# Trailing the transposes of GpSimd's products by one unit, and moving the initial chunks' product to another PSUM bank and another engine, in a hybrid decoder block

## The chip, the core and the metric

One core of one Trainium2 chip runs the whole program in one launch, in float32. The metric is the device time of one execution in microseconds (us). The core has a matrix engine (TensorE, PE in the profile, with its weight loads as PEld), a vector engine (VectorE, DVE), an activation engine (ScalarE, ACT), a general-purpose engine (GpSimd, POOL) and an engine that only issues transfers here (SyncE, SP). Each engine works through its own instructions strictly in order and waits on semaphores for the others.

## The reference

The input `x` is 1 x 2048 x 1024. Sixteen learned meta tokens are put in front, and one layer is computed:

```
h    = concat(meta, x)
proj = rmsnorm(h) @ w_in                       # 1024 -> 1024, columns split in two
u    = proj[:, :512]   -> 32 groups x 16 ch    # S5: 64 complex states a group
v    = proj[:, 512:]   -> 4 groups x 128 ch    # trailing means over 2/4/8/16 positions
s_t  = A s_{t-1} + B u_t ;  y = Re(C s) + d*u  # per group, A diagonal and complex
ys   = gelu(y) * sigmoid(gelu(y) @ glu_w + glu_b)
yp   = ((mean_w(v) - v) @ pool_w) * pool_scale
h    = h + concat(rmsnorm(ys), rmsnorm(yp)) @ w_out
h    = h + (silu(n2 @ w_gate) * (n2 @ w_up)) @ w_down      # n2 = rmsnorm(h), FF 2816
out  = rmsnorm(h), meta tokens dropped
```

## The kernel before

**Tiling.** The 2048 positions are two halves (`b` = 0, 1) of 128 chunks of T = 8 consecutive positions. A slice is one position of every chunk of a half: 128 rows, so there are 8 slices a half, and a 17th slice with the 16 meta tokens. In the program's text slices 1 and 2 are projected first, then slice 0 (the meta tokens), then 3 to 16. Products with large weights are made in float32r: each operand is split into a high and a low part (`split`, L107) and three matmuls stand for one (`mm3`, L116 to L119). So a line of the profile with `pj`, L117 to L119, is a matmul of the input projection.

**The recurrence.** The 32 S5 groups are handled in 8 units of 4 groups (`UG` = 4, `NU` = 8). With chunks of 8 positions, a unit needs four tables, which are built on the chip from the parameters and parked in DRAM as `pk_d[u]`, 2568 columns wide:

- columns 0 to 511: the matrices that lead from a chunk's inputs to its state. GpSimd multiplies them out (`ptp`, L551: two products and a sum in `outer`), TensorE transposes them (`pp`, L564), ScalarE copies the bank (`pst`, L566), SP sends it off (L567);
- columns 512 to 1023: `n9`, from the state to the outputs, multiplied out by VectorE (L550), sent off by L552;
- columns 1024 to 1535: the product within a chunk. TensorE makes `kp` from `n9` (L556), ScalarE copies it to `ks` (L559), VectorE adds the diagonal (L560), SP writes it to a padded array in DRAM (L561), and eight transfers read it back shifted (L569);
- the rest: cosines and sines `tb`, begun by four small GpSimd copies (L573 to L576) and doubled by VectorE in `grow` (L578).

That is `units()`. It is a generator, and so is `params()` ahead of it, which prepares the small parameter tables: `advance(2)` takes two steps of them before each slice of the first half (L633 to L639), so that TensorE has projections beside the building of the tables. All temporaries of `units()` have one buffer, but for `n9` and `tb` with two.

**The second stage.** When all tables are built, their SBUF is handed back (`par.close()`, L642), `pool_block(0)` forms the trailing means with GpSimd sums and one VectorE operation (L727) a group, and `ssm_unit(0, u)` runs the recurrence of one unit on the first half, unit by unit, while the 8 slices of the second half are projected (L734 to L740). In `ssm_unit`: load `pk` (L661); for the first half, the product of the two meta chunks, `pv0` (two columns a group, L677), copied by VectorE to `sm` (L678), combined into the initial state `z[:, :, 0]` (L679 to L681); then the product of the 128 chunks, `pvs` (L686); a rotation (L689), the scan (L691), a rotation back in which GpSimd takes two multiplications (L695), and the output product `py` (L700, L701), read by ScalarE with GELU (L704).

**Banks.** PSUM has eight banks in three rings: `tr` (2, transposes), `mm` (4, the projection and later matmuls) and `s` (2). In the first half `kp` and `pp` share the `s` ring; in the second stage `pv0`, `pvs` and `py` share it.

**The order of the work.** The program's text is not the order on the engines: before the launch a planner sorts each engine's instructions by their place in the text and by when its own cost model thinks that they are ready. That order is then fixed. A matmul that waits for another engine holds up every matmul that the planner put behind it.

Of the kernel before, what the change touches and what calls it, by code (L numbers as in the profile page):

```python
# [16 lines left out]
P = 128  # L17
# [5 lines left out]
H = 16  # L23
# [4 lines left out]
UG = 4  # L28
NU = G // UG
# [8 lines left out]
def kernel(  # L38
# [9 lines left out]
    V, A, GP, PE, SY = nc.vector, nc.scalar, nc.gpsimd, nc.tensor, nc.sync  # L48
# [9 lines left out]
    pk_d = [dram.tile([P, PKN], F32, name=f"pk_d{u}") for u in range(NU)]  # L58
# [13 lines left out]
    def tr_tile(nm):  # L72
        return ps_tr.tile([P, 4, P], F32, name=nm, tag="tr")

    def mm_tile(nm):
        return ps_mm.tile([P, 512], F32, name=nm, tag="mm")

    def s_tile(nm):
        return ps_s.tile([P, 512], F32, name=nm, tag="s")

    def g4(ap):
        return ap.rearrange("p (g k) -> p g k", g=UG)

    def tt(o, a, b, op, e=V):
        e.tensor_tensor(o, a, b, op=op)  # L85
# [36 lines left out]
    ident = const.tile([P, P], F32, name="ident")  # L122
# [29 lines left out]
    def yview(b):  # L152

        return xu[b].rearrange("c g t h -> c (g t h)").rearrange("c (k t e) -> c k t e", k=4, t=T)
# [352 lines left out]
    def grow(ct, st, w1, w2, n, ck, sk, e1, e2):  # L507

        lo, hi = slice(0, n), slice(n, 2 * n)
        sh = [P, ct.shape[1], n]  # L510
        ck = ck.unsqueeze(2).to_broadcast(sh)
        sk = sk.unsqueeze(2).to_broadcast(sh)
        w1, w2 = w1[:, :, :n], w2[:, :, :n]
        tt(ct[:, :, hi], ct[:, :, lo], ck, M_, e1)
        tt(w1, st[:, :, lo], sk, M_, e1)
        tt(ct[:, :, hi], ct[:, :, hi], w1, S_, e1)
        tt(st[:, :, hi], st[:, :, lo], ck, M_, e2)
        tt(w2, ct[:, :, lo], sk, M_, e2)
        tt(st[:, :, hi], st[:, :, hi], w2, A_, e2)
# [11 lines left out]
    def units():  # L531
        unit_p = par.enter_context(tc.tile_pool(name="unit", bufs=1))

        def pu_(shape, nm, bufs=None):
            return unit_p.tile(shape, F32, name=nm, tag=nm, bufs=bufs)

        for u in range(NU):
            gs = slice(u * UG, (u + 1) * UG)
            n9 = pu_([P, UG, 9, H], "n9", 2)
            n9t = pu_([P, UG, 9, H], "n9t")  # L540
            ptp = pu_([P, UG, 8, H], "ptp")
            ptt = pu_([P, UG, 8, H], "ptt")

            def outer(o, tmp, xp, xq, yp, yq, K, e):
                sh = [P, UG, K, H]
                tt(o, xp[:, gs, :K].unsqueeze(3).to_broadcast(sh), yp[:, gs].unsqueeze(2).to_broadcast(sh), M_, e)
                tt(tmp, xq[:, gs, :K].unsqueeze(3).to_broadcast(sh), yq[:, gs].unsqueeze(2).to_broadcast(sh), M_, e)
                tt(o, o, tmp, A_, e)

            outer(n9, n9t, xa1, xa2, zv[0], zv[1], 9, V)  # L550
            outer(ptp, ptt, xr1, xr2, y1, y2, 8, GP)  # L551
            SY.dma_start(pk_d[u][:, 512:1024].rearrange("p (g k) -> p g k", g=UG),  # L552
                         n9[:, :, 1:].rearrange("p g k h -> p g (k h)"))
            kp = g4(s_tile("kp"))
            for i in range(UG):
                PE.matmul(kp[:H, i], y1[:, u * UG + i], n9[:, i, :8].rearrange("p k h -> p (k h)"),  # L556
                          start=True, stop=True)
            ks = pu_([H, UG, P], "ks")
            A.copy(ks, kp[:H])  # L559
            tt(ks[:, :, :H], ks[:, :, :H], dg[:, gs], A_)  # L560
            SY.dma_start(kpad_d[gs, :, P:].rearrange("g h e -> h g e"), ks)  # L561
            pp = g4(s_tile("pp"))
            for i in range(UG):
                PE.transpose(pp[:, i], ptp[:, i].rearrange("p k h -> p (k h)"), ident)  # L564
            pst = pu_([P, UG, P], "pst")
            A.copy(pst, pp)  # L566
            SY.dma_start(pk_d[u][:, :512].rearrange("p (g k) -> p g k", g=UG), pst)  # L567
            for j in range(8):
                SY.dma_start(pk_d[u][j * H:(j + 1) * H, 1024:1536].rearrange("h (g k) -> h g k", g=UG),  # L569
                             kpad_d[gs, :, P - j * H:2 * P - j * H].rearrange("g h e -> h g e"))  # L570
            tb = pu_([P, 2, UG, NCH + 1], "tb", 2)
            tw = pu_([P, 2, UG, 64], "tw")
            GP.tensor_copy(tb[:, 0, :, :NE], eb[:, 0, gs])  # L573
            GP.tensor_copy(tb[:, 1, :, :NE], eb[:, 1, gs])
            GP.tensor_copy(tb[:, 0, :, NCH], cA[:, 8, gs])
            GP.tensor_copy(tb[:, 1, :, NCH], sA[:, 8, gs])  # L576
            for k in range(4, 7):
                grow(tb[:, 0], tb[:, 1], tw[:, 0], tw[:, 1], 1 << k, cA[:, k + 1, gs], sA[:, k + 1, gs], V, V)  # L578
            SY.dma_start(pk_d[u][:, 1536:], tb.rearrange("p q g c -> p (q g c)"))
            yield  # L580


    banks = [mm_tile(f"pj{q}") for q in range(4)]
# [64 lines left out]
    def rotate(o, tmp, vv, cc, sg, sign, eng=V):  # L648

        tt(o, vv, cc, M_)  # L650
        tt(tmp[:S], vv[S:], sg[S:], M_, eng)
        tt(tmp[S:], vv[:S], sg[:S], M_, eng)
        tt(o, o, tmp, A_ if sign > 0 else S_)
# [3 lines left out]
    def ssm_unit(b, u):  # L657
        g0 = u * UG
        gs = slice(g0, g0 + UG)
        pk = ss_p.tile([P, PKN], F32, name="pk", tag="pk", bufs=2)  # L660
        SY.dma_start(pk, pk_d[u])  # L661
        pm, nm, mm = g4(pk[:, :512]), g4(pk[:, 512:1024]), g4(pk[:, 1024:1536])
        ct, sg = g4(pk[:, 1536:2052]), g4(pk[:, 2052:2568])
        if u % 2 == 0:
            us8[0] = ss_p.tile([P, 2 * UG, NCH], F32, name="us", tag="us", bufs=2)
            for h in range(2):
                pu = tr_tile("put")
                for i in range(UG):
                    PE.transpose(pu[:, i], xu[b][:, g0 + h * UG + i].rearrange("c t h -> c (t h)"), ident)
                A.copy(us8[0][:, h * UG:(h + 1) * UG], pu)  # L670
        us = us8[0][:, (u % 2) * UG:(u % 2 + 1) * UG]
        z = ss_p.tile([P, UG, NCH + 1], F32, name="z", tag="z", bufs=2)
        sm = ss_p.tile([P, 4, UG], F32, name="sm", tag="sm", bufs=2)
        if b == 0:
            pv0 = g4(s_tile("pv0"))
            for i in range(UG):
                PE.matmul(pv0[:, i, :2], pm[:, i], um_sb[:, g0 + i], start=True, stop=True)  # L677
            V.tensor_copy(sm[:, 2:4], pv0[:, :, :2].rearrange("p g c -> p c g"))  # L678
            rotate(sm[:, 0], sm[:, 1], sm[:, 2], ct[:, :, 1], sg[:, :, 1], 1)  # L679
            tt(sm[:, 0], sm[:, 0], r8[:, gs], M_)  # L680
            tt(z[:, :, 0], sm[:, 0], sm[:, 3], A_)  # L681
        else:
            V.tensor_copy(z[:, :, 0], carry[:, gs])
        pv = g4(s_tile("pvs"))
        for i in range(UG):
            PE.matmul(pv[:, i], pm[:, i], us[:, i], start=True, stop=True)  # L686
        wr = ss_p.tile([P, UG, NCH], F32, name="wr", tag="wr")
        tmp = ss_p.tile([P, UG, NCH], F32, name="tmp", tag="tmp", bufs=2)
        rotate(wr, tmp, pv, ct[:, :, 1:], sg[:, :, 1:], -1)  # L689
        for i in range(UG):  # L690
            V.tensor_tensor_scan(z[:, i, 1:], r8[:, g0 + i:g0 + i + 1].to_broadcast([P, NCH]), wr[:, i],  # L691
                                 z[:, i, 0:1], op0=M_, op1=A_)
        st = ss_p.tile([P, UG, NCH], F32, name="st", tag="st")
        tmp2 = ss_p.tile([P, UG, NCH], F32, name="tmp2", tag="tmp", bufs=2)
        rotate(st, tmp2, z[:, :, :NCH], ct[:, :, :NCH], sg[:, :, :NCH], 1, GP)  # L695
        if b == 0:
            rotate(carry[:, gs], sm[:, 1], z[:, :, NCH], ct[:, :, NCH], sg[:, :, NCH], 1)
        py = s_tile("py")
        for i in range(UG):
            PE.matmul(py[:, i * P:(i + 1) * P], us[:, i], mm[:, i], start=True, stop=False)  # L700
            PE.matmul(py[:, i * P:(i + 1) * P], st[:, i], nm[:, i], start=False, stop=True)  # L701
        c0 = u % 2 * UG * H
        yv = yview(b)[:, u // 2][:, :, c0:c0 + UG * H].rearrange("c t (i h) -> c t i h", h=H)
        A.activation(yv, py.rearrange("c (i t h) -> c t i h", i=UG, t=T), AF.Gelu_apprx_tanh)  # L704
# [26 lines left out]
    for _ in pool_block(0):  # L731
        pass
    ssm_unit(0, 0)
    for u in range(NU):  # L734
        j = T + 1 + u
# [469 lines left out]
    g = 0  # L1205
# [60 lines left out]
```

## Time and profile before

| | |
|---|---|
| median of 3 executions (lowest to highest) | 1859.86 us (1859.7 to 1863.04) |
| the profiled execution | 1853.8 us |
| its span, first to last instruction | 1851.9 us |
| mean granted TensorE clock | 0.991 |
| busy: DVE, POOL, ACT | 1234.0, 813.3, 673.1 us |
| DMA | 298.36 MB, mean 161 GB/s |

The profile comes from one execution. A row of the timeline gives the start and length of an instruction, engine, line, what it writes and reads, and in square brackets how long the engine had been idle before it and whose end released it. A row of the waits gives engine, line and tile that waited, who ended the wait, the total in us, how often, and the longest. A row of the windows gives, for a stretch of the span, its length, the busy time (and count of instructions) of PE, PEld, DVE, ACT and POOL, the granted clock as a share of full speed, the DMA share and GB/s.

### The profile page before, as it was taken

What the parts mean: (1) busy time and instruction counts of PE and PEld (TensorE: products, weight loads), DVE (VectorE), ACT (ScalarE), POOL (GpSimd) and SP (SyncE); (2) the same over time, 40 slices, a digit from 0 to 9 for tenths busy, and PEclk for the clock granted to TensorE, in tenths of its full rate; (3) what the DMA queues carried; (4) which work ended last, traced back from release to release, by engine and by line L of the source; (5) the groups of instructions that cost most, each with busy time, mean ns of one, the idle gap of its engine ahead of it and who ended that gap; (6) DMA issues with size and microseconds to landing.
All of it is one profiled execution on the core that took longest, in us unless ns stands there. A gap on an engine that the chain in (4) does not pass through costs nothing.

```text
span 1851.9 us, 23672 instructions
## 1 busy us (share of the span) xinstructions
PE 1795.5 (97%) x8497; PEld 1491.6 (81%) x8497; DVE 1234.0 (67%) x1913; ACT 673.1 (36%) x1213; POOL 813.3 (44%) x619
## 2 busy tenths in 40 slices
PE   7999997999999999999999999999999999999998
PEld 6777886888887788888887788888888888888886
DVE  6995777766467876666667867776776444445763
ACT  5332334433455333333334333333333343333341
POOL 1774425633354465454657866665662000003400
PEclk9999998999999999999999999999999999999999
DMA  6355425444355344443436554554447765536771
GB/s 185 93 160 177 155 98 187 158 150 143 116 181 165 108 158 144 142 159 108 159 121 205 194 179 154 165 183 152 137 153 229 236 196 173 159 114 208 247 222 70
DMA packets 260517, 298.36 MB, mean 161 GB/s; under 512 B 17148, under 2 KB 204048, under 8 KB 255536
## 3 DMA queue, kind: packets, MB, share of 16 engines
q1 hardware_dynamic: 260304, 296.84, 50.5%
q8 instruction: 67, 1.10, 0.2%
q14 instruction: 50, 0.41, 0.1%
q0 software_dynamic: 96, 0.01, 0.0%
HBM read 202.37 MB, written 96.53 MB: 161 GB/s over the span
## 4 chain that ended last, share of the span: by engine, by line
PE 58%; issue 13%; DMA 7%; DVE 6%; POOL 3%; ACT 1%; POOLq 0%; SPq 0%; DVEq 0%; ACTq 0%
PE pr L117 13%; PE pr L118 13%; PE pr L119 13%; PE po L117 2%; PE po L119 2%; PE po L118 2%; PE pd L118 2%; PE pd L119 2%; PE pd L117 2%; DMA hd<-h_d 2%; DMA c<-c_d 1%; DVE wcl L85 1%; DMA out_dram<-c 1%; PE pj L119 1%; PE pj L117 1%
## 5 line engine op out<-in xcount | busy, mean ns | idle before, releaser
L85 DVE TENSOR_TENSOR wcl<-raw,wch 128x512 fp32r<-128x512 f32 x176 | 179.1, 1020 | 34.4 <-ACT wch L110 33.4
L110 ACT CAST wch<-raw 128x512 fp32r<-128x512 f32 x176 | 108.7, 622 | 255.2 <-PE pr L118 227.5
L85 DVE TENSOR_TENSOR fl<-fr,fh 128x512 fp32r<-128x512 f32 x168 | 115.1, 697 | 122.3 <-ACT fh L110 122.1
L110 ACT CAST fh<-fr 128x512 fp32r<-128x512 f32 x168 | 96.0, 584 | 193.1 <-PE pd L118 167.3
L110 ACT CAST wch<-s 128x512 fp32r<-128x512 f32 x132 | 82.0, 622 | 221.6 <-PE pr L118 168.7
L85 POOL TENSOR_TENSOR s<-raw 128x512 f32<-128x512 f32 x44 | 66.8, 1518 | 168.3 <-DVE wcl L85 74.1
L85 DVE TENSOR_TENSOR wcl<-s,wch 128x512 fp32r<-128x512 f32 x132 | 122.5, 928 | 23.2 <-ACT wch L110 23.1
L85 POOL TENSOR_TENSOR db22h<-db22h,hd 128x512 f32<-128x512 f32 x4 | 5.2, 1294 | 251.5 <-DVE db22h L85 251.5
L117 PE MATMUL po<-wh,mh 128*128 128x512 f32 x256 | 103.9, 406 | 2.9 <-ACT mh L767 2.9
L117 PE MATMUL pj<-wh,xh 128*128 128x512 f32 x256 | 103.3, 411 | 2.3 <-ACT xh L110 2.3
L118 PE MATMUL pj<-wl,xh 128*128 128x512 f32 x256 | 102.6, 403 | 0.0
L119 PE MATMUL pj<-wh,xl 128*128 128x512 f32 x256 | 102.4, 405 | 0.0
L119 PE MATMUL po<-wh,ml 128*128 128x512 f32 x256 | 100.7, 394 | 0.0
L118 PE MATMUL po<-wl,mh 128*128 128x512 f32 x256 | 100.7, 393 | 0.0
L85 POOL TENSOR_TENSOR rs<-rv,mhalf 128x1 f32<-128x1 f32 (+2 forms) x35 | 32.0, 914 | 152.6 <-DVE rv L91 143.4
L85 POOL TENSOR_TENSOR wr<-wr 128x512 f32<-128x512 f32 x44 | 67.0, 1523 | 66.8 <-DMA wr<-in_w_down_dram 61.3
L85 DVE TENSOR_TENSOR gt<-gt,ut 128x512 f32<-128x512 f32 x88 | 92.8, 1056 | 0.0
L85 POOL TENSOR_TENSOR ut<-gt 128x512 f32<-128x512 f32 x22 | 34.2, 1555 | 106.6 <-DVE gt L85 106.6
L85 POOL TENSOR_TENSOR tmp<-z,pk 64x512 f32<-64x512 f32 x32 | 49.0, 1531 | 71.4 <-issue 57.5
L85 DVE TENSOR_TENSOR gt<-pr,gt 128x512 f32<-128x512 f32 x66 | 45.4, 689 | 50.7 <-PE pr L119 50.3
L1017 ACT ACTIVATE gt<-gt 128x512 f32<-128x512 f32 x88 | 55.5, 632 | 53.4 <-DVE gt L85 53.4
L117 PE MATMUL pr<-xt2h,wch 128*128 128x512 f32 x176 | 68.8, 391 | 6.1 <-DVE gt L85 3.5
(394 smaller groups left out, 5550.8 us busy)
## 6 DMA issues: line engine op xcount, KB each, us to landing
fr<-ff_d SPq DMA_DIRECT2D x56, 704.0 KB, 5.0
raw<-in_w_gate_dram SPq DMA_DIRECT2D x44, 512.0 KB, 4.9
raw<-in_w_up_dram SPq DMA_DIRECT2D x44, 512.0 KB, 4.5
ff_d<-gt SPq DMA_DIRECT2D x22, 1024.0 KB, 3.9
pk<-pk_d SPq DMA_DIRECT2D x16, 1284.0 KB, 6.2
ff_d<-ut SPq DMA_DIRECT2D x22, 768.0 KB, 5.4
wr<-in_w_down_dram SPq DMA_DIRECT2D x22, 512.0 KB, 3.3
wd_d<-wr SPq DMA_DIRECT2D x22, 512.0 KB, 3.6
```

Source lines behind the costliest of these rows:

```text
L85: e.tensor_tensor(o, a, b, op=op)
L110: A.copy(hi, src)
L117: PE.matmul(o, lh, rh, start=first, stop=False)
L118: PE.matmul(o, lh, rl, start=False, stop=False)
L119: PE.matmul(o, ll, rh, start=False, stop=last)
L1017: lambda i, j: A.activation(gt[:, i, j], gt[:, i, j], AF.Silu), b == 0 and f0 == 0)
```

## The change

In `units()` the four transposes, the copy and the transfer of a unit's GpSimd product become a function `turn_p`. Unit u calls it for the product of unit u-1; the last product is turned after the loop, with one more step of the generator. For this the product `ptp` has two buffers in place of one. In `ssm_unit` the product of the meta chunks `pv0` takes a bank of the ring `mm` in place of `s`, and ScalarE copies it to `sm` in place of VectorE.

```
+        def turn_p(u, ptp):
+
+            pp = g4(s_tile("pp"))
+            for i in range(UG):
+                PE.transpose(pp[:, i], ptp[:, i].rearrange("p k h -> p (k h)"), ident)
+            pst = pu_([P, UG, P], "pst")
+            A.copy(pst, pp)
+            SY.dma_start(pk_d[u][:, :512].rearrange("p (g k) -> p g k", g=UG), pst)
+
+        was = None
         for u in range(NU):
...
-            ptp = pu_([P, UG, 8, H], "ptp")
+            ptp = pu_([P, UG, 8, H], "ptp", 2)
...
             SY.dma_start(kpad_d[gs, :, P:].rearrange("g h e -> h g e"), ks)
-            pp = g4(s_tile("pp"))
-            for i in range(UG):
-                PE.transpose(pp[:, i], ptp[:, i].rearrange("p k h -> p (k h)"), ident)
-            pst = pu_([P, UG, P], "pst")
-            A.copy(pst, pp)
-            SY.dma_start(pk_d[u][:, :512].rearrange("p (g k) -> p g k", g=UG), pst)
+            if u:
+                turn_p(u - 1, was)
+            was = ptp
...
             yield
+        turn_p(NU - 1, was)
+        yield
...
-            pv0 = g4(s_tile("pv0"))
+            pv0 = g4(mm_tile("pv0"))
...
-            V.tensor_copy(sm[:, 2:4], pv0[:, :, :2].rearrange("p g c -> p c g"))
+            A.copy(sm[:, 2:4], pv0[:, :, :2].rearrange("p g c -> p c g"))
```

## The prediction

> **What bounds the kernel now.** I read the page's first part, then the windows around the two places that the change touches, then TensorE's waits there, and only then single rows.
>
> ```profile
> span 1851.9 us, 23672 instructions
> PE 1795.5 (97%) x8497; PEld 1491.6 (81%) x8497; DVE 1234.0 (67%) x1913; ACT 673.1 (36%) x1213; POOL 813.3 (44%) x619
> ```
>
> TensorE is busy 97% of the span, so a gain must be idle or slow TensorE time. The stretches that matter are the building of the tables (60 to 142 us), what is left of the first half (142 to 158), the first units of the recurrence (158 to 211) and the rest of it (211 to 290):
>
> ```profile
> 60.00:142.00 82.00, 75.69 (x384) 59.82 (x384) 75.82 (x196) 28.89 (x50) 62.03 (x71) 0.95 0.49 146
> 142.00:158.00 16.00, 16.00 (x83) 13.38 (x81) 2.02 (x6) 4.28 (x8) 0.55 (x1) 1.00 0.55 164
> 158.00:211.00 53.00, 46.59 (x262) 39.53 (x261) 44.98 (x75) 16.69 (x28) 35.27 (x28) 0.97 0.46 163
> 211.00:290.00 79.00, 79.00 (x466) 68.93 (x467) 56.19 (x126) 25.80 (x42) 17.98 (x15) 1.00 0.31 111
> ```
>
> TensorE idles 6.31 us in the first stretch and 6.41 in the third, and not at all in the second and fourth, so what it has won by 211 us is kept to 290. But in the first stretch VectorE is busy 75.82 of 82 us and in the third 44.98 of 53: a second engine stands close behind TensorE in both places where TensorE waits. The waits, first from 60 to 160 us, then from 150 to 290:
>
> ```profile
> PE pp L564 <- POOL ptp L85: 6.3, 2, 5.0
> ```
>
> ```profile
> PE pvs L686 <- DVE sm L678: 5.8, 2, 3.4
> PE pv L677 <- POOL sum L85: 0.4, 1, 0.4
> ```
>
> The change aims at the first two. Together they are 12.1 us, 0.65% of the span.
>
> **Part one, the trailing transposes.** Per unit the same four transposes, one copy and one transfer remain; they move behind `kp` of the next unit on TensorE, behind the next `ks` copy on ScalarE, and on SP behind the unit's own eight `kpad_d` reads and its `tb`. What the removed wait was worth:
>
> ```profile
> 94.47 1.11 PE L564 MATMUL pp<-ident,ptp 128*128 128x128 f32 x4 [4.96 <-POOL ptp L85]
> 130.47 0.66 PE L564 MATMUL pp<-ident,ptp 128*128 128x128 f32 x4 [1.36 <-POOL ptp L85]
> ```
>
> ```profile
> 95.00:100.00 5.00, 5.00 (x16) 3.93 (x15) 3.09 (x3) 1.06 (x2) 4.92 (x4) 0.53 0.29 60
> ```
>
> After the 4.96 us gap the granted clock is 0.53 for the whole of the next five us, which loses 5 x 0.47 = 2.4 us (the four transposes there take 1.11 us, after the short gap 0.66). So the ceiling of this part is 4.96 + 2.4 + 1.36 = 8.7 us.
>
> Does GpSimd's product really come in time when the transposes trail? The late product and why it was late:
>
> ```profile
> 87.53 5.16 POOL L85 TENSOR_TENSOR ptp<-xr,y 128x512 f32<-128x512 f32 x1
> 92.77 1.66 POOL L85 TENSOR_TENSOR ptp<-ptp,ptt 128x512 f32<-128x512 f32 x1
> ```
>
> ```profile
> POOL ptp L85 <- PE pp L564: 7.5, 3, 4.1
> ```
>
> The product ended at 94.43 and `pp` started at 94.47. From unit 2's `pp` (94.47) to unit 6's (130.47) are 36 us, 9 a unit, so a product that is turned one unit later is ready even where it takes 5.16 us. GpSimd also loses its own 7.5 us of waiting for the single buffer. I take the whole wait as gone from `pp`, at no cost for the second buffer.
>
> What is late next? VectorE and, behind it, SP. VectorE's idle time in this stretch that GpSimd caused, the last table, and the way from it to the first `pk`:
>
> ```profile
> 100.61 0.23 DVE L85 TENSOR_TENSOR tb<-tb,cA 128x64 f32<-128x64 f32 x1 [2.49 <-POOL tb L573]
> 128.79 0.23 DVE L85 TENSOR_TENSOR tb<-tb,cA 128x64 f32<-128x64 f32 x1 [1.65 <-POOL tb L573]
> 129.21 1.29 DVE L85 TENSOR_TENSOR tb<-tb,cA 128x64 f32<-128x64 f32 x1
> 142.28 0.20 DVE L85 TENSOR_TENSOR ks<-ks,dg 16x64 f32<-16x64 f32 x1
> ```
>
> ```profile
> 145.07 0.38 SPq L561 DMA_DIRECT2D kpad_d<-ks  x1
> 149.17 5.00 SPq L569 DMA_DIRECT2D pk_d<-kpad_d  x8
> 154.29 0.51 SPq L661 DMA_DIRECT2D pk<-pk_d  x1
> ```
>
> ```profile
> 160.72 1.02 PE L677 MATMUL pv<-um_sb,pk 128*128 128x2 f32 x8 [0.41 <-POOL sum L85]
> ```
>
> The first `pk` is issued at 154.29 behind the last eight reads and is needed at 160.72, where TensorE already waits 0.41 us; the sums named there are no operand of this matmul, so I read it as the landing of `pk`. If TensorE arrives 8.7 us sooner and `pk` does not, it stands there. How much sooner can `pk` come? At most by VectorE's two waits, 2.49 + 1.65 = 4.1 us; at least 0, since SP issues without a pause from 149.17 to 154.29. I take 3, nearer the ceiling, because the 7.5 us that GpSimd no longer waits lie ahead of both `tb` copies. The trailing means need only the last slice of the first half, so their first sum and VectorE's first operation on it move into the empty 142 to 158 stretch, which keeps them out of the way of unit 0. Part one: 3 us, bounds 0 and 8.7.
>
> **Part two, `pv0`.** The rows at its two waits, TensorE's first and then VectorE's:
>
> ```profile
> 177.71 0.49 PE L686 MATMUL pvs<-us,pk 128*128 128x128 f32 x2 [2.46 <-DVE sm L678]
> 178.35 0.79 PE L701 MATMUL py<-pk,st 128*128 128x128 f32 x2 [0.15 <-DVE st L85]
> 181.49 0.91 PE L686 MATMUL pvs<-us,pk 128*128 128x128 f32 x6
> 210.83 1.16 PE L686 MATMUL pvs<-us,pk 128*128 128x128 f32 x8 [3.38 <-DVE sm L678]
> 211.82 0.60 PE L229 MATMUL ptv<-ident,vs 128*128 128x128 f32 x4
> ```
>
> ```profile
> 177.57 0.73 DVE L85 TENSOR_TENSOR st<-st,tmp 128x512 f32<-128x512 f32 x1
> 182.44 0.69 DVE L85 TENSOR_TENSOR wr<-pvs,pk 128x512 f32<-128x512 f32 x1 [1.52 <-PE pvs L686]
> 201.67 1.23 DVE L94 SCALAR_TENSOR_TENSOR pt<-sum,vt 128x1024 f32<-128x1024 f32 x1 [1.98 <-POOL sum L85]
> 210.69 0.68 DVE L85 TENSOR_TENSOR xl<-pt,xh 128x512 fp32r<-128x512 f32 x1
> ```
>
> With a bank of its own, `pv0` no longer stands before `pvs`. But in the same order the next matmul is `py` L701, which needs `st`, and VectorE ends that at 177.57 + 0.73 = 178.30. So the first wait mostly changes its name: TensorE does `pvs` in it (about 1 us) and then waits until 178.3. What is won is that `pvs` is done before `py` and not after it, so VectorE's 1.52 us before `wr` goes. At 210.83 the next in line is `ptv`, which needs a `tr` bank that VectorE's `xl` frees at 210.69 + 0.68 = 211.37; it started at 211.82, so 0.4 us are won of 3.38. The copies:
>
> ```profile
> L678 DVE COPY sm<-pv x8: 155/158/168, 161.8 to 269.3; 128x8 f32<-128x8 f32 x8
> ```
>
> ```profile
> L259 ACT COPY um_sb<-ptm x1: 213/213/213, 58.6 to 58.6; 128x64 f32<-128x64 f32 x1
> ```
>
> Eight copies of 0.158 us leave VectorE, three of them (units 1 to 3) in the stretch that it bounds: 0.5 us. ScalarE gets eight of at most 0.213, beside 16.69 busy us in 53; behind them wait evacuations of the projection. The bank taken from `mm` costs at worst that the projection waits out one such copy a unit, 8 x 0.213 = 1.7 us; no row shows TensorE waiting for that ring in these stretches, and the copy is released by TensorE's own last `pv0` matmul, so I take nothing. Part two: 1.5 + 0.4 + 0.5 = 2.4 us. Bounds: -1.7, and above all idle of both waits, 2.46 + 0.15 + 3.38 = 6.0, plus the slow clock after the first:
>
> ```profile
> 175.00:180.00 5.00, 2.39 (x12) 1.96 (x11) 4.81 (x14) 0.00 (x0) 4.11 (x4) 0.82 0.34 107
> 180.00:185.00 5.00, 5.00 (x27) 4.53 (x27) 3.42 (x5) 1.87 (x3) 4.13 (x4) 0.83 0.42 145
> ```
>
> The clock lost is 5 x 0.18 + 5 x 0.17 = 1.7 us: 7.7 in all. The Trainium skill, "TensorE: Matmul & The Clock Gate", section "HAM oscillation", wants idle gaps of more than about 3.4 us before the clock is halved: by it this wait of 2.46 us would have cost no clock and the ceiling would be 6.0; the trace agrees for the gap of 4.96 us and speaks against it here.
>
> **The sum.** 3 + 2.4 = 5.4 us. Against the profiled execution, 1853.8 (its span of 1851.9 and 1.9 around it), that gives 1848.4. The median of the runs is 6.1 above that execution, so I take the difference from the median: 1859.86 - 5.4 = 1854.5 us. What a measurement of this kernel tells from no change is about 0.2%, 3.7 us.
>
> **Rivals.**
>
> *The lead is swallowed (no change).* VectorE has 6.2 us to spare in the first 82, and part of its busy time is not work: the same `tb` form takes 0.23 us at 128.79 and 1.29 at 129.21, with GpSimd at work on a product. If GpSimd's earlier products only hold VectorE at other places, `pk` comes when it came, TensorE stands in front of `pv0` for what it won, and GpSimd's sums (the 1.98 us at 201.67) hold the third stretch. For it: VectorE's 75.82 of 82 us; against it: the 4.1 us are idle, not slow. It gives 0 to -2, about 1858.9. The Trainium skill, "SBUF — State Buffer", section "SBUF: two separate sides", has GpSimd and a VectorE operation with two SBUF inputs exclude each other for a whole instruction; by that rule earlier products win VectorE nothing, and this rival is the outcome. The 1.29 us agrees with it.
>
> *Everything counts.* The planner, with other arrival times, puts more projections in front of the first `pv0` and of `py`, and both waits vanish with their slow clock: 8.7 + 7.7 = 16.4, so 1843.5. Against it: `st` and `xl` are where the waits would move in the present order.
>
> *Slower.* The copy target `pst` still has one buffer. Products 6 and 7 are now turned close together, after unit 7's `kp`. The rows of unit 6's `pst` now, on ScalarE and SP:
>
> ```profile
> 131.21 0.59 ACT L566 COPY pst<-pp 128x512 f32<-128x512 f32 x1 [0.17 <-PE pp L564]
> 140.38 0.59 ACT L566 COPY pst<-pp 128x512 f32<-128x512 f32 x1 [0.39 <-DMA pk_d<-pst]
> ```
>
> ```profile
> 138.12 0.37 SPq L567 DMA_DIRECT2D pk_d<-pst  x1
> ```
>
> ```profile
> DMA to landing us min/median/max: 2.0/2.3/5.9
> ```
>
> The copy of 131.21 is issued only at 138.12, because SP is filled with the reads, and the copy of 140.38 already waits for its landing (the last row: 2.0 to 5.9 us for these transfers). Trailing, unit 6's goes out at about 145.5 and unit 7's follows it behind the eight reads, at 154.2. If the second stage's memory waits for that landing too, the first `pk` slips by 0.4 of issue and 2.0 to 5.9 of landing, 2.4 to 6.3, in the middle 4.4; with a slow clock as priced above, 2.4, and less part two, 4.4 + 2.4 - 2.4 = +4.4: 1864.3. It decides from the point where unit 7's `pst` lands after the first `pk` could have been issued.
>
> **How the numbers follow.** Forecast 0.50 (own range -2 to -9, of which 0.08 lie within 3.7 us of no change), swallowed 0.25, everything 0.08, slower 0.17. Faster by over 0.2%: 0.42 + 0.08 = 0.50; within: 0.08 + 0.25 = 0.33; slower: 0.17. The range leaves out the outer end of "everything" and the upper part of "slower": 1848.5 to 1864.
>
> **What would show it.** Right: `pp` no longer waits for `ptp`, and the granted clock from 95 to 100 us is full; VectorE's `tb` waits shrink; the first `pk` is issued about 3 us sooner and TensorE waits longer for it at `pv`; `pvs` waits for no `sm`, but `py` L701 waits for `st` and `ptv` for `xl`. Wrong: `pk` at its old place (swallowed), TensorE without a wait from 60 to 211 (everything), ScalarE idle at `pst` for its transfer (slower), or a difference that arises behind 290 us, where this sum expects none.

## The result, and the profile after

| | before | after |
|---|---|---|
| median of 4 executions | 1861.39 us (1859.7 to 1863.04) | 1887.41 us (1885.35 to 1887.5) |
| the profiled execution, its span | 1853.8, 1851.9 us | 1887.5, 1885.7 us |
| mean granted TensorE clock | 0.991 | 0.983 |

The change makes the kernel slower by 26.0 us: ratio 1.0137, 95% interval 1.0125 to 1.0149. The forecast was 5.4 us faster, and 1887 lies above the whole range.

The two spans differ by 33.8 us, more than the medians, because the profiled execution of before lies 7.6 us below its median. A part of that is seen early: unit 0's `kp` (its second four matmuls; from here on, unit 0's `kp`) starts at 74.4 us before and at 77.7 after, 3.3 us later, with nothing of the change ahead of it but the second buffer. I take 3.3 us off where I compare places in the two traces. The first output matmul `po` comes at 303.7 and 333.2: 29.5 - 3.3 = 26.2 us later, the whole loss. So it arises before `po`, in the stretches that the change touches.

The first part of the page of after, as that of before was shown, and the windows of the same four stretches (length, busy time and count of PE, PEld, DVE, ACT, POOL, the granted clock, DMA share, GB/s):

```profile
span 1885.7 us, 23673 instructions
PE 1808.4 (96%) x8497; PEld 1500.9 (80%) x8497; DVE 1251.2 (66%) x1905; ACT 672.9 (36%) x1221; POOL 805.9 (43%) x619
```

```profile
60.00:142.00 82.00, 74.82 (x416) 58.80 (x415) 80.02 (x190) 25.03 (x47) 56.67 (x68) 1.00 0.43 131
142.00:158.00 16.00, 12.86 (x64) 10.22 (x62) 6.71 (x27) 5.27 (x10) 2.15 (x5) 1.00 0.57 171
158.00:211.00 53.00, 37.32 (x167) 31.81 (x168) 35.34 (x57) 11.28 (x22) 31.22 (x26) 0.71 0.48 159
211.00:290.00 79.00, 75.50 (x429) 65.19 (x428) 44.84 (x99) 24.59 (x46) 15.49 (x14) 0.98 0.29 101
```

The building of the tables went as hoped for TensorE's clock (1.00, before 0.95), but VectorE is busy 80.02 of 82 us, before 75.82. The damage is in the next two rows: TensorE idles 15.68 us from 158 to 211 (before 6.41) and 3.14 from 142 to 158 (before none), and its clock is 0.71 in the third stretch (before 0.97). That is 9.3 + 3.1 + 53 x 0.26 = 26 us. With the other two rows (0.9 and 3.5 us more idle time, 82 x 0.05 = 4.1 of clock won in the first and 79 x 0.02 = 1.6 lost in the fourth) it is 28 of the 29.5 us, roughly, since the clock is a mean over idle time too and a row doesn't hold the same work in both.

TensorE's waits from 60 to 160 us, then from 150 to 290:

```profile
PE kp L566 <- ACT ks L569: 4.4, 4, 1.7
PE ptv L229 <- ACT vs L226: 3.8, 1, 3.8
PE pj L119 <- DVE xl L85: 2.7, 2, 1.7
PE pp L541 <- ACT ks L569: 1.1, 1, 1.1
```

```profile
PE py L710 <- DVE st L85: 9.1, 3, 5.6
PE pv L686 <- POOL sum L85: 4.7, 1, 4.7
PE ptv L229 <- ACT vs L226: 4.6, 2, 3.8
PE pt L181 <- ACT us L679: 2.4, 1, 2.4
```

Both waits that the change aimed at are gone: `pp` waits for no product (once, 1.1 us, for ScalarE's `ks`) and `pvs` for no `sm`. Others have their place, 12.0 us in the first rows and 20.8 in the second, with the 3.8 in both. The tail of the trailing shows on four engines. Rows of the timelines of ScalarE, SyncE, GpSimd and TensorE:

```profile
157.08 0.58 ACT L543 COPY pst<-pp 128x512 f32<-128x512 f32 x1 [6.24 <-DMA pk_d<-pst]
157.56 0.59 ACT L110 CAST xh<-pt 128x512 fp32r<-128x512 f32 x1
159.09 0.69 ACT L226 ACTIVATE vs<-pj,rs 128x512 f32<-128x512 f32 x1
```

```profile
156.37 5.01 SPq L576 DMA_DIRECT2D pk_d<-kpad_d  x8
161.48 0.53 SPq L544 DMA_DIRECT2D pk_d<-pst  x1
163.84 0.79 SPq L670 DMA_DIRECT2D pk<-pk_d  x2
```

```profile
164.03 2.17 POOL L85 TENSOR_TENSOR sum<-vt 128x910 f32<-128x910 f32 x2 [4.02 <-DMA pk_d<-pst]
179.26 2.86 POOL L85 TENSOR_TENSOR sum<-sum 128x774 f32<-128x774 f32 x2 [7.38 <-DMA p_d<-pt]
```

```profile
159.83 0.66 PE L229 MATMUL ptv<-ident,vs 128*128 128x128 f32 x4 [3.85 <-ACT vs L226]
164.68 1.97 PE L181 MATMUL pt<-ident,xs 128*128 128x128 f32 x8 [2.40 <-ACT us L679]
171.37 1.84 PE L686 MATMUL pv<-um_sb,pk 128*128 128x2 f32 x8 [4.73 <-POOL sum L85]
175.69 1.66 PE L686 MATMUL pv<-um_sb,pk 128*128 128x2 f32 x7
```

ScalarE stands 6.24 us for the transfer that empties the single `pst`; behind that copy wait `xh`, then `vs`, and `ptv` on TensorE. Unit 7's own transfer leaves at 161.48, behind the eight reads of `kpad_d`; the second stage's first sum and `us` wait until it has landed, and the first `pk` is loaded at 163.84 (before 154.29; 6.2 us later when the 3.3 are off). The last fence holds a second fact: in it stand all of TensorE's rows from 159.8 to 175.7 us but four (two of `put`, one each of `pvs` and `py`), and none of the projection. Slice 8's last `pj` ends at 156.0 and slice 9's first starts at 177.4.

### The profile page after: what moved, and what is told of

Same layout as the page of the kernel before. It is cut to its first block, busy times and chain, and to the rows that moved or that the text cites. A ratio compares the mean times of both kernels' runs of the same rounds, so it can differ in the third digit from the quotient of the medians.

```text
span 1885.7 us, 23673 instructions
## 1 busy us (share of the span) xinstructions
PE 1808.4 (96%) x8497; PEld 1500.9 (80%) x8497; DVE 1251.2 (66%) x1905; ACT 672.9 (36%) x1221; POOL 805.9 (43%) x619
## 4 chain that ended last, share of the span: by engine, by line
PE 72%; DVE 14%; DMA 6%; POOL 3%; issue 2%; ACT 2%; SPq 1%; DVEq 0%; POOLq 0%; ACTq 0%
PE pr L117 13%; PE pr L118 13%; PE pr L119 13%; PE pd L118 6%; PE pd L119 6%; PE pd L117 6%; PE po L117 2%; PE po L119 2%; PE po L118 2%; DVE tb L85 1%; DMA c<-c_d 1%; DVE z L700 1%; DVE wcl L85 1%; PE pj L117 1%; PE pj L118 1%
```

## The experiments

Three theories were stated first. T: the tail of the trailing transposes, as above. R: the place of `pv0` in the projection's ring. In the text `ssm_unit(0, 0)` and `ssm_unit(0, 1)` stand ahead of `proj_slice(9)`, and unit u+1 ahead of slice 9+u; so in one ring slice 9 has its banks behind two `pv0`, which need tables from DRAM. C: ScalarE's copy, in order ahead of evacuations. Ratios below are to the kernel before, run beside each on the same chip.

**The parts alone.** `e1_trail_only` leaves out part two, `e2_pv0_only` part one, `e3_bank_only` moves only the bank, `e4_copy_only` only the copy:

```
e1  after, with   pv0 = g4(s_tile("pv0"))  and  V.tensor_copy(sm[:, 2:4], ...)
e2  before, with  pv0 = g4(mm_tile("pv0")) and  A.copy(sm[:, 2:4], ...)
e3  before, with  pv0 = g4(mm_tile("pv0"))
e4  before, with  A.copy(sm[:, 2:4], ...)
```

> Only the trailing transposes; pv0 as in the kernel before. Theory R (ring order): the loss of 26 us comes from pv0 asking for its bank in the projection's ring, because the planner hands out the banks of a ring in the order of the text and so puts no matmul of slice 9 ahead of the first pv0. It expects this run within 8 us of before (1852 to 1870): faster by the pp waits (up to 8.7), slower where ScalarE stands for the single pst and the second stage waits for the last product's landing. Theory T (tail of the trailing): the landing of the last product holds the second stage and everything behind it; it expects most of the loss here, 1875 to 1890. Theory C (in-order ScalarE copy): no change here beyond 4 us.

> Only pv0: bank of the projection's ring and ScalarE's copy; transposes as before. Theory R: most of the loss, 1878 to 1890, with no matmul of the projection between the end of slice 8 and the first pv0. Theory T: within 5 us of before. Theory C: slower too, so this run alone does not part R and C.

> Only the bank of pv0 moves to the projection's ring; VectorE still copies it. Theory R: as slow as with both, 1878 to 1890. Theory C: as before, within 4 us of 1861. Theory T: as before.

> Only the copy of pv0 moves to ScalarE; the bank stays in the small ring. Theory R: within 4 us of before (1857 to 1865); TensorE's wait for sm shrinks and the waits for st and xl appear. Theory C: slower by 10 us or more. Theory T: as before.

| | median us | ratio, interval |
|---|---|---|
| e1_trail_only | 1873.53 | 1.0073 (1.0052 to 1.0095) |
| e2_pv0_only | 1880.43 | 1.0110 (1.0093 to 1.0126) |
| e3_bank_only | 1883.96 | 1.0127 (1.0112 to 1.0142) |
| e4_copy_only | 1864.24 | 1.0016 (1.0007 to 1.0025) |

The bank alone costs 1.27%, 23.6 us, nearly the whole loss; the trailing alone 0.73%, 13.6 us, more than R had said and less than T. They don't add up (37 against 26): both make TensorE stand at the same place, before the first `pv0` (5.00 us in `e1_trail_only`). The copy costs 0.16%, 3 us, so C falls. TensorE's rows in `e3_bank_only`, which has neither the trailing nor ScalarE's copy, then ScalarE's and VectorE's of slices 8 and 9:

```profile
159.99 0.66 PE L181 MATMUL pt<-ident,xs 128*128 128x128 f32 x4 [0.19 <-ACT us L670]
165.19 1.84 PE L677 MATMUL pv<-um_sb,pk 128*128 128x2 f32 x8 [4.54 <-issue]
166.88 2.06 PE L686 MATMUL pvs<-us,pk 128*128 128x128 f32 x8
169.39 1.87 PE L677 MATMUL pv<-um_sb,pk 128*128 128x2 f32 x8
173.46 0.77 PE L117 MATMUL pj<-wh,xh 128*128 128x512 f32 x1
```

```profile
150.72 0.69 ACT L219 ACTIVATE xu<-pj,rs 128x512 f32<-128x512 f32 x1 [1.51 <-PE pj L119]
156.58 0.69 ACT L226 ACTIVATE vs<-pj,rs 128x512 f32<-128x512 f32 x1 [1.36 <-PE pj L119]
154.21 0.69 DVE L85 TENSOR_TENSOR xl<-pt,xh 128x512 fp32r<-128x512 f32 x1 [4.28 <-ACT xh L110]
```

TensorE stands 4.54 us before the first `pv0`, and slice 9's projection begins only when both `pv0` are through. It lacks neither a bank nor its operands: ScalarE has emptied slice 8's two banks at 151.4 and 157.3, and VectorE has split the last of slice 9's operands at 154.9. It stands behind both `pv0` in TensorE's order. `e2_pv0_only` shows the same, with no matmul of the projection from 155.0 to 171.5. In the trace of before the projection's matmuls run on between `pv0` of unit 0 (160.72) and that of unit 1 (168.73).

**The tail.** `e5_trail_pst2` gives `pst` two buffers, `e7_trail_lastnow` turns unit 7's product in its own step, `e13_lastnow_pst2` does both. All are `e1_trail_only` otherwise.

```
e5   pst = pu_([P, UG, P], "pst", 2)
e7   was = ptp
     if u == NU - 1:
         turn_p(u, ptp)          # and no turn_p behind the loop
e13  both
```

> The trailing alone (pv0 in its old bank, copied by VectorE: 1873.5 us, 0.73% over the kernel before) with two buffers of pst instead of one. In the trailing alone ScalarE's copy of unit 7's turned product stood 5.95 us for the DMA that empties pst, and 5 us later SyncE issued the product's own DMA and 2.3 us after that the first load of pk. Theory P (one buffer: the single pst is what makes the tail expensive): the copy of unit 7 no longer waits, its DMA and the first pk load come 5 to 6 us sooner, the memory's sum is not held, and the time falls to that of before or below it, 1857 to 1863 us. Theory L (late order: unit 7's product is turned and stored behind the eight reads of kpad and the store of tb in every queue, with or without a free buffer): the copy of pst no longer waits but the first pk load moves by less than 2 us, the pv of unit 0 stays near 169 us, and the time stays at 1870 to 1876 us.

> The trailing alone, except that unit 7's product is turned in its own step, right behind unit 6's, so that there is no tail behind the loop; units 0 to 6 trail as in the change. Theory P (single pst): two turned products follow each other through one buffer still, ScalarE waits 2 to 6 us at the second copy for the DMA of the first, but now ahead of the eight reads of kpad, so SyncE, which issues in order, has the reads later; pk comes about where the trailing alone has it, 1868 to 1875 us. Theory L (late order): the store of unit 7's product leaves ahead of the reads of kpad as in the kernel before, the first pk load is back near 154 to 156 us, and the time is 1856 to 1864 us. If the trailing of units 0 to 6 itself costs or gains something, it shows here as the distance from the kernel before: my prediction's part one had a gain of 3 us for it.

> The trailing alone with both mends of its tail: unit 7's product turned in its own step, and two buffers of pst, so that the two products at the end don't wait for each other's DMA. pv0 stays in its old bank with VectorE. My prediction's part one had a gain of 3 us for the trailing, and the tail alone was what hid it: 1856 to 1860 us. If the trailing gains nothing even so (TensorE's lead at unit 3 is given back because it then waits for ScalarE's ks and the projection's operands): 1860 to 1864 us.

| | median us | ratio, interval | first `pk` load after unit 0's `kp` |
|---|---|---|---|
| before | | | 154.29 - 74.4 = 79.9 us |
| e1_trail_only | 1873.53 | 1.0073 (1.0052 to 1.0095) | 161.50 - 78.9 = 82.6 |
| e5_trail_pst2 | 1863.52 | 1.0019 (1.0010 to 1.0028) | 158.97 - 77.3 = 81.7 |
| e7_trail_lastnow | 1862.22 | 1.0007 (0.9995 to 1.0020) | 155.73 - 74.3 = 81.4 |
| e13_lastnow_pst2 | 1862.48 | 0.9999 (0.9986 to 1.0011) | 159.75 - 78.1 = 81.7 |

Either mend takes most of the loss away: 0.19% and 0.07% are left of 0.73%. Unit 7's transfer leaves at 159.14 in `e1_trail_only`, behind all eight reads; at 150.53 in `e5_trail_pst2`, ahead of them; and at 150.87 in `e7_trail_lastnow`, behind three. So the loss needs both, one buffer and a last product turned behind the loop. In `e7_trail_lastnow` ScalarE still waits 6.01 us for `pst`, and it costs nothing that can be measured; the wait itself is not the price. Nor is the late `pk`: by the last column the mends bring it only 0.9 to 1.2 us forward, not the 5 to 6 us that theory P had for `e5_trail_pst2`, and TensorE still stands 4.2 to 4.4 us before the first `pv0`. Where the rest of the loss lies is told further down. With both mends the trailing is worth nothing: 0.9999, where I had 3 us.

Why nothing, `e13_lastnow_pst2` shows. Its TensorE is freer while the tables are built, and stands before `pv0` instead:

```profile
60.00:142.00 82.00, 77.63 (x421) 61.10 (x421) 79.34 (x193) 26.24 (x49) 62.83 (x71) 0.98 0.47 135
```

```profile
166.10 1.83 PE L686 MATMUL pv<-um_sb,pk 128*128 128x2 f32 x8 [4.41 <-issue]
```

VectorE is full, though its wait for GpSimd's `tb` fell from 4.1 us to 1.7. Groups of its instructions from the first `kp` to the last `ks`, in before and then in `e13_lastnow_pst2` (count, busy us, mean ns, idle before):

```profile
L85 DVE TENSOR_TENSOR tb<-tb,cA 128x128 f32<-128x128 f32 x15 | 8.1, 541 | 0.0
L85 DVE TENSOR_TENSOR n<-xa,z 128x576 f32<-128x576 f32 x6 | 4.7, 790 | 0.2 <-PE kp L556 0.2
L85 DVE TENSOR_TENSOR tw<-tb,sA 128x64 f32<-128x64 f32 x14 | 2.5, 211 | 0.0
L85 DVE TENSOR_TENSOR tb<-tb,cA 128x64 f32<-128x64 f32 x12 | 4.5, 374 | 4.1 <-POOL tb L573 4.1
```

```profile
L85 DVE TENSOR_TENSOR tb<-tb,cA 128x128 f32<-128x128 f32 x16 | 10.4, 648 | 0.0
L85 DVE TENSOR_TENSOR n<-xa,z 128x576 f32<-128x576 f32 x6 | 6.0, 1006 | 0.0
L85 DVE TENSOR_TENSOR tw<-tb,sA 128x64 f32<-128x64 f32 x14 | 4.5, 350 | 0.1
L85 DVE TENSOR_TENSOR tb<-tb,cA 128x64 f32<-128x64 f32 x13 | 5.3, 410 | 1.7 <-POOL tb L582 1.7
```

The same operations on the same shapes take longer (790 to 1006 ns, 541 to 648, 211 to 350), others a little less (the 128x256 forms 482 to 411). The long ones stand beside GpSimd's products. In `e13_lastnow_pst2` a `tb` of 128x128 takes 0.27 to 0.32 us at ten places and 1.14 to 1.38 at six, and each of the six ends 0.14 or 0.15 us behind a GpSimd product, as in this pair:

```profile
137.39 1.42 POOL L85 TENSOR_TENSOR ptp<-ptp,ptt 128x512 f32<-128x512 f32 x1
137.59 1.37 DVE L85 TENSOR_TENSOR tb<-tb,cA 128x128 f32<-128x128 f32 x1
```

The wait became busy time, and from the first `kp` (72.8 and 76.5) to VectorE's last `ks` operation (142.28 and 147.02) it is 69.5 us before and 70.5 with the trailing.

**The bank: place or amount?** `e12_held_only` is before with one bank of the ring held for all `pv0`; `e8_held_bank` is after with that, `e11_held_lastnow` adds the mend of `e7_trail_lastnow`. `e14_bank_first2` and `e15_bank_from2` move the bank for units 0 and 1, or for 2 to 7, alone.

```
e8, e11, e12  pvall = ps_mm.tile([P, 512], F32, name="pvall", tag="mm")   # ahead of the first half's loop
              V.memset(pvall, 0.0)
              ...
              pv0 = pvall[:, u]
e14           pv0 = g4(mm_tile("pv0") if u < 2 else s_tile("pv0"))
e15           pv0 = g4(s_tile("pv0") if u < 2 else mm_tile("pv0"))
```

> The kernel after, except that pv0 of all eight units lie in one bank of the projection's ring that is taken and zeroed by VectorE once before the loop over the units; so pv0 asks for no bank in the ring any more, the projection keeps one bank fewer for good, and ScalarE copies as in the change. Theory R (ring order: pv0 asked for a bank in the projection's ring ahead of the projection's next tiles, so slice 9 could not start until pv0 of the first two units had begun): the projection's matmuls of slice 9 run again ahead of the first pv0, and the time is that of the trailing alone plus at most the 0.2% of ScalarE's copy, 1871 to 1878 us. Theory B (a bank fewer: the projection wants every bank that it has): the time stays at 1885 us or goes above, 1883 to 1890 us.

> The kernel after with both mends: pv0 of all units in one bank taken once ahead of the loop, and unit 7's product turned in its own step. Theories R and L together: both losses are gone, what is left is ScalarE's copy (0.16% alone, 3 us) less what the trailing of units 0 to 6 gains, 1856 to 1866 us. Theory B or P: one of the losses stays, 1870 to 1886 us.

> The kernel before, except that pv0 of all eight units lie in one bank of the projection's ring, taken and zeroed by VectorE once before the loop over the units; the copy stays with VectorE and the transposes don't trail. Theory R (ring order is what the bank costs): pv0 no longer stands in the ring ahead of the projection's slices, and the time is within 0.3% of before, 1859 to 1867 us. Theory B (a bank fewer): the projection, left with three banks of four for the rest of that stage, pays as with the bank moved alone (1884 us), 1875 to 1885 us. A value between the two gives each its share: the held bank has the price of a bank fewer, the rest of the 23 us is the order.

> The kernel before, except that pv0 of units 0 and 1 alone are in the projection's ring; those of units 2 to 7 stay in their old bank, and VectorE copies all of them. Theory R, as read from the trace of after (the projection stands still from 158 to about 180 us because slice 9's tiles come behind the pv0 of units 0 and 1): nearly all of the 23 us that the moved bank costs alone is in these two, 1876 to 1885 us. If instead each of the eight pv0 holds up the projection by a like amount, two of eight cost 6 us: 1865 to 1869 us.

> The counterpart: units 2 to 7 in the projection's ring, units 0 and 1 in their old bank. Theory R with the loss at the start: 1861 to 1868 us. With a like amount for each pv0, six of eight: 1876 to 1881 us.

| | median us | ratio, interval |
|---|---|---|
| e8_held_bank | 1878.65 | 1.0097 (1.0081 to 1.0113) |
| e11_held_lastnow | 1870.66 | 1.0058 (1.0044 to 1.0072) |
| e12_held_only | 1878.13 | 1.0089 (1.0076 to 1.0102) |
| e14_bank_first2 | 1872.20 | 1.0051 (1.0035 to 1.0066) |
| e15_bank_from2 | 1883.11 | 1.0114 (1.0101 to 1.0127) |

The times did not settle it. The held bank costs 0.89% by itself, but I took it ahead of the first half's loop, so the projection is a bank short there too: from 100 to 142 us TensorE is busy 36.23 us at a clock of 0.92 (before 40.64 at 1.00), and the first `pk` is loaded at 162.58. So its time shows what a bank fewer costs with the tables' stretch included, and not what `pv0` costs by its place. Its trace says more. With the bank held, slice 9 runs ahead of the first `pv0` again: ScalarE empties the bank of its first half at 160.88, and the `pv0` comes at 168.66. And from the first `pk` load to the first `po` it is 149.4 us before, 155.8 with a bank held and 167.7 in `e3_bank_only`: a bank fewer costs 6.4 us of this stretch, the moved bank 18.2. Within the held bank the mend of the tail is worth 0.39% (e8 against e11). Units 0 and 1 alone cost 9.5 us and units 2 to 7 alone 21.2, so neither form of what I expected holds, neither "all at the start" nor "a like amount each". The trace of `e15_bank_from2` has the reason:

```profile
173.23 0.47 PE L119 MATMUL pj<-wh,xl 128*128 128x512 f32 x1
193.75 1.71 PE L677 MATMUL pv<-um_sb,pk 128*128 128x2 f32 x8
197.03 0.77 PE L117 MATMUL pj<-wh,xh 128*128 128x512 f32 x1
```

The `pv0` at 193.75 is unit 2's. Slice 9 runs as before and slice 10 stands from 173.7 to 197.0 behind it. Whichever `pv0` is the first in the ring stops the projection there.

**The place alone.** `e18_slice_first` is before with the text swapped so that slice 9+u stands ahead of unit u; `e19_slice_first_bank` is that with the bank moved. `e10_pv0_tr` is before with `pv0` in the ring of the transposes.

```
e18, e19     for u in range(NU):          # and no ssm_unit(0, 0) ahead
                 ...
                 proj_slice(j)
                 ssm_unit(0, u)
e19          pv0 = g4(mm_tile("pv0"))
e10          pv0 = tr_tile("pv0")
```

> The kernel before with one swap in the program's text: slice 9+u of the projection comes ahead of unit u of the recurrence instead of behind units u and u+1. It is the base for the next kernel. With it alone: between 1855 and 1875 us, no theory speaks to it.

> The swapped text, with pv0 of all units moved to the projection's ring (VectorE copies). Theory R (place: the bank costs 23 us because in the program's text pv0 of units u and u+1 stand ahead of slice 9+u in the same ring, so that the projection waits for tables that come from DRAM): now the projection's tiles come first, TensorE does slice 9 while pk loads, and the move costs at most 6 us over the kernel with the swap alone. Theory B (amount: with pv0 in it the ring of four is a bank short, wherever pv0 stands; a bank held for the whole stage alone cost 15 to 16 us): 13 to 20 us over the kernel with the swap alone.

> The kernel before with pv0 in the ring of the transposes, which has two banks, instead of the recurrence's; VectorE copies. The recurrence's ring gets the same relief as in the change and the projection keeps its four banks. Theory R and B agree that the projection's own slices run on ahead of the first pv0; what they leave open is whether the transposes of the slices' operands, which then stand behind pv0 in their ring, hold the projection up. If they don't, what was hoped of the bank comes: pvs no longer waits for VectorE's sm, 1857 to 1861 us; if they do, 1866 to 1880 us.

| | median us | ratio, interval |
|---|---|---|
| e18_slice_first | 1876.03 | 1.0074 (1.0057 to 1.0091) |
| e19_slice_first_bank | 1879.95 | 1.0097 (1.0082 to 1.0112) |
| e10_pv0_tr | 1863.47 | 1.0015 (1.0001 to 1.0029) |

With the slices ahead, the bank costs 3.9 us by the medians instead of 23.6, and the executions of the two kernels overlap (1873.3 to 1878.8 and 1876.5 to 1881.2): R. The base is another kernel, so this by itself would not exclude that the swap hides a part of the price; the two traces above, of slice 9 held up with banks free and of the held bank, speak against it. The windows from 158 to 180 us, first of `e3_bank_only`, then of `e19_slice_first_bank`:

```profile
158.00:180.00 22.00, 16.24 (x73) 13.68 (x71) 13.69 (x28) 5.07 (x8) 10.28 (x9) 0.77 0.57 197
```

```profile
158.00:180.00 22.00, 22.00 (x114) 18.31 (x113) 5.33 (x13) 5.15 (x9) 9.60 (x9) 1.00 0.65 219
```

TensorE is full where it stood. The swap itself costs 14.9 us, most of it after the first `po`, as I take it because the recurrence starts later, which is not shown; so it is a test and no mend. `e10_pv0_tr` gives the recurrence's ring the same relief without touching the projection, and gains nothing: 0.15% slower at the middle of its interval.

None of the fifteen kernels is faster than before beyond its interval.

## Why the prediction was wrong

**The step that failed most** is in part two: "The bank taken from `mm` costs at worst that the projection waits out one such copy a unit, 8 x 0.213 = 1.7 us; no row shows TensorE waiting for that ring in these stretches, ... so I take nothing." The bank costs 23.6 us alone, and in `e3_bank_only` TensorE makes no matmul of the projection from 156.6 to 173.5 us. I priced how long a bank is occupied and left out in which order it is asked for and what its user waits for. That no row showed a wait for the ring was true of a ring in which only the projection stood. Two facts of the kernel before would have told it: slice 9 has its banks behind two `pv0` in the text, and `pv0` needs `pk`, from DRAM. With the first `pk` issued at 154.29 and `pv0` at 160.72, TensorE, which by the windows had no idle time from 142 to 158, would have nothing to do for some microseconds.

**The rival "slower" had its mechanism right in part, and too little weight.** ScalarE idle at `pst` (6.24 us), unit 7's transfer behind the reads, the memory held for it, `pk` 6.2 us later in after and 2.7 in `e1_trail_only` (I had 2.4 to 6.3, and the mended kernels have 1.5 to 1.8 of it too): each is in the trace. Its price of 4.4 + 2.4 = 6.8 us for the trailing was half of the 13.6 measured. By the first `po`, `e1_trail_only` is 6.0 us behind before (314.2 - 303.7, less 4.5 at unit 0's `kp`). The other part, 8.7 us, arises between the first `po` and the first `pr`, a matmul of the feed-forward part (272.3 us against 263.6). TensorE's order is another one there: behind the first `po`, before, `e5_trail_pst2`, `e7_trail_lastnow` and `e13_lastnow_pst2` have the same order for 45 us and need 263.4 to 265.1 us to `pr`, while `e1_trail_only` has the first eight `ppool` ahead of every `py`, and its `pgate` waits 4.7 us for ScalarE (1.9 before). So as far as the first `po` the rival's price is near what was lost, and more than half of the loss lies behind it; that later matmuls would come in another order stood in neither the sum nor the rivals, and whether the order is the whole of the 8.7 us no run shows. I had the rows for this rival in hand, and set it at 0.17 while the forecast took the opposite for `pk`.

**Part one's 3 us are nothing** without the tail, which is the rival *swallowed*. What I held against it, that VectorE's 4.1 us were "idle, not slow", was wrong: they went from idle to slow. That agrees with the Trainium skill, "SBUF — State Buffer", section "SBUF: two separate sides", whose rule I had cited for the rival: the wait shrank, and two-operand forms stretched to the end of a GpSimd product. No run here tried GpSimd's products in other places.

**Part two's copy** went as the text said for the waits and not for the gain. TensorE's waits in `e4_copy_only`, 150 to 290 us:

```profile
PE py L701 <- DVE st L85: 4.3, 2, 2.8
PE ptv L229 <- DVE xl L85: 1.7, 1, 1.7
```

They are the two that I named, 6.0 us for the 5.8 at `pvs`. So the wait changed its name whole, and the 1.5 + 0.4 + 0.5 us that I kept of it were not there: 1.3 to 4.7 us slower by its interval.

**Right:** `pp` without a wait for `ptp` and the full clock from 95 to 100 us; VectorE's wait at `tb` shorter (1.7 us for 4.1); `pvs` without a wait for `sm`; in the whole change, nearly no difference behind the first stages.

## What to carry to other kernels

A tile moved to another ring of PSUM is asked for in that ring's order: look at which tiles of the ring come behind it in the text and at what the moved tile's writer waits for, before pricing how long it sits there. When a step is made to trail, the last one trails into the next stage: follow its copy, its buffer and its transfer past everything already queued there. A wait of TensorE is worth only what the next thing on its path lets through; here it was VectorE's tables, whose time did not change.

## What the runs showed of the hardware

Windows of after (PE busy and count, the granted clock, DMA share, GB/s) behind the waits of 3.85, 2.40 and 4.73 us:

```profile
160.00:165.00 5.00, 2.36 (x14) 0.60 0.60 180
165.00:170.00 5.00, 1.65 (x8) 0.50 0.95 348
170.00:175.00 5.00, 3.63 (x17) 0.50 0.97 308
175.00:180.00 5.00, 4.87 (x17) 0.50 0.29 89
180.00:185.00 5.00, 5.00 (x24) 0.85 0.00 0
```

The clock stays at 0.50 to 0.60 for some 20 us, as long as waits follow each other, where the single 4.96 us wait of before was followed by one stretch of five at 0.53. And a transfer soon behind large ones is late. The first `p_d` of after is issued at 169.2 us, 5 us behind two loads of `pk` of 1284 KB each, and releases GpSimd's next sum at 179.26, 10 us later, after 7.38 us of idle time. Before, it is issued at 163.16, 7.5 us behind the last of those loads, and the sum runs at 166.83, 3.7 us later, after 1.45 us. The other traces agree: 9.7 and 9.6 us from issue to sum where `p_d` leaves 3.7 and 1.9 us behind the loads (`e1_trail_only`, `e7_trail_lastnow`), 3.7 us where it leaves 8.4 and 8.6 us behind (`e5_trail_pst2`, `e13_lastnow_pst2`). `e7_trail_lastnow` has the same 7.38 us of idle time on GpSimd and loses nothing by it.
